# Where the fetched rows' sums begin and leave, and when the odd mixer's weights are asked for, in a two-layer decoder trunk

## The chip, the cores and the metric

The kernel runs on one core of a Trainium2 chip. The metric is the device time of one execution in microseconds (us). Repeated executions of this kernel agree within a few tenths of a microsecond, so a change of 0.2% (3 us) can be told from no change.

## The reference, cut to what matters

Two pre-norm residual layers over 256 tokens of width 1024. Layer 0 mixes tokens by attention and retention, layer 1 by a gated short convolution. After each mixer comes PEER, an expert mixer: every token picks 8 x 16 = 128 of 16,384 experts, and each expert is one row of `u` and one row of `v`.

```python
for layer in range(2):
    xn = rmsnorm(h, norm_mix[layer])
    h = h + (attn_retention_mixer if layer == 0 else short_conv_mixer)(xn, ...)
    h = h + peer(rmsnorm(h, norm_ffn[layer]), peer_w_q[layer], ..., peer_u[layer], peer_v[layer])
return rmsnorm(h, final_norm)

def peer(t, w_q, sub_keys, u, v):
    ...                                   # product keys: eidx (token, 128 experts), gate
    hid = gelu(einsum('td,tkd->tk', t, u[eidx]))
    return einsum('tk,tkd->td', gate * hid, v[eidx])
```

## The kernel before, in words

**Two ways through PEER.** The last 160 tokens (`TD`) take a dense way: all 16,384 experts are run over them, 128 tiles of `u` and then 128 tiles of `v`, each tile 128 experts by 1024 floats, and a matrix of gates zeroes what a token did not choose. The first 96 tokens (`TG`) take a fetched way: class `Gather` reads exactly the chosen rows from HBM by indirect DMAs on the POOL queue (L966). One such DMA fetches one row of 1024 floats for each of 128 partitions. 96 tokens x 128 experts are 96 DMAs of rows of `u` and 96 of rows of `v` in each layer; the text calls the result of one such DMA "a row". Partitions 0 to 95 hold one token each. Partitions 96 to 127 (`TG:`) help out: in the first 32 rows they work for tokens 0 to 31, in the next 32 for tokens 32 to 63, in the last 32 for tokens 64 to 95.

**The sums of the fetched way.** VectorE (DVE) consumes rows in order (`consume`, called from `step`). A row of `v` is scaled and added into `acc[q]`, q = 0, 1, 2 for the three blocks of 32 rows (L985 for the first row, L987 and L988 for the first of a later block, L991 for all others). `acc[q][:TG]` begins on `acc[q-1][:TG]`. The helpers' sums, `acc[q][TG:]`, are carried to their tokens' place in `acc[0]` by a small DMA on the POOL queue (`part`, L1003), the third of them after the very last row. Then `fold` (L999) adds `acc[2][:TG]` and `acc[0][:TG]` into the residual `h[:TG]`, two DVE instructions, the second of which waits for that DMA.

**The v stage** is the loop `for i in range(NK)` at the end of `peer`: 128 steps, one tile of `v` (`pv`) each, eight PSUM banks `vo[b]` that collect the dense tokens' output. In 33 steps the raw tile is multiplied in float32 (L1484, 16 matmul instructions). In the 95 steps of `SPL` it is split beforehand into a rounded part `vhi` on ScalarE (ACT, L1369) and a rest `vlo` on DVE (L1376), three steps ahead, with the gated activations split likewise (L1442, L1443, L1450), and the step is L1488 and L1490. Tile 126 is raw, tiles 123, 124, 125 and 127 are split.

**The pace of the rows.** In each step `ga.step()` adds `ga.rate` to a credit and consumes a row per whole credit; after each consume the next row is asked for, up to six ahead. The rate is chosen so that `(16 - end) * late` rows are left when step 114 begins, and from there it is `late` rows a step:

```python
late = 1.0 if last else 0.8
end = 3.5 if last else 7.5
ga.rate = (ga.TOTAL - ga.c - (16 - end) * late) / (NK - 16.0)
```

`last` is layer 1, the last one.

**The end of the v stage in layer 0.** At step 123 (`NK - 5`) all rows must be consumed and `fold` is called on DVE. At step 126 (`NK - 2`), ahead of that step's own products, PE adds the transposed `h[:TG]` to the banks as eight products with the identity (L1476), and ACT copies them to `XT` (L1479), the transposed residual. After step 127 `fold(b)` takes the dense tokens' sums out of the banks (ACT L1497, DVE L1498), and `Folded.folded` makes the odd mixer's input from `XT`.

**The end in layer 1** is `Final.folded`: eight `fold(b)`, sixteen transposes back to token rows (L506), squares on ACT (L586), the gather's `fold` on DVE (L999), two copies of the dense tokens of the first half into `h` (L603), gains (L583), the norm (L365 to L377), the scaling (L592, L590) and four stores (L593). It calls `ga.fold()` in its middle.

**The stream of weights.** `Stream` keeps eight raw buffers for all weight tiles of the program, in one order: `wq`, `pu`, `pv` of layer 0, then the odd mixer's `ow_in` and `ow_out`, then layer 1. A tile is asked for when the tile eight places earlier has been handed out (`free(self.nl - RAW)`), so the odd mixer's first tiles (numbers 128 and on, counted from the first tile of `pv`) are asked for in the last steps of layer 0's v stage. All loads go out on SP's queue (L131) but for every second `pv` tile, which goes on ACT's. In the program each load waits for the release of the buffer that it goes into. Instructions of one engine or queue run in the order in which the program writes them.

The functions that the diff touches, before:

Of the kernel before, what the change touches and what calls it, by code (L numbers as in the profile page):

```python
# [19 lines left out]
P = 128  # L20
# [8 lines left out]
NK = 128  # L29
# [40 lines left out]
def shape_constants():  # L70
    c = np.zeros((P, C_N), np.float32)
    c[:, C_ID:C_ID + P] = np.eye(P)
    c[:, C_IO:C_IO + P] = np.arange(P)[None, :]
    c[:, C_ONE] = 1.0
    c[:, C_ST:C_ST + TK] = np.array(STARTS)[None, :]
# [29 lines left out]
class Stream:  # L105
# [58 lines left out]
    def ahead(self, extra=0):  # L164
        n = len(self.srcs)
        while True:
            if self.nl < n and self.free(self.nl - RAW):
                self._load()
            elif self.ns < min(n, self.nu + extra + self.depth()) and self.ns < self.nl:
                self._split()  # L170
            else:
                return

    def parts(self):

        self._split()
        while self.nl < len(self.srcs) and self.free(self.nl - RAW):
# [14 lines left out]
def trunk_kernel(ctx, tc, x, small, cst, mcst, ew_in, ew_out, ow_in, ow_out, wq, keys, pu, pv, pun, gains, out):  # L192
# [363 lines left out]
    class Final(Sums):  # L556
# [12 lines left out]
        def folded(self, XT, fold, ga):  # L569


# [7 lines left out]
            def row(a):  # L579
                return fq[a] if a > 1 else h[:, 0, a * 512:(a + 1) * 512]  # L580

            def gained(a):
                v.tensor_tensor(part(a), row(a), self.g[:, a % 2 * 512:(a % 2 + 1) * 512], OP.mult)  # L583

            def square(a):
                act.activation(junk, row(a), AF.Square, accum_out=self.w[:, a // 2, a % 2:a % 2 + 1])  # L586
# [10 lines left out]
            for a in (2, 3, 0, 1):  # L597
                back(fq[a], XT, a // 2, a % 2)
            for a in (2, 3):
                square(a)  # L600
            ga.fold()
            for a in range(2):
                v.tensor_copy(h[TG:, 0, a * 512:(a + 1) * 512], fq[a][TG:, :])  # L603
# [12 lines left out]
            gained(1)  # L616
# [54 lines left out]
    def even_mixer(before, norm):  # L671
        with tc.tile_pool(name=nm("mix"), bufs=1) as mp, tc.tile_pool(name=nm("mix2"), bufs=2) as mp2:
# [152 lines left out]
            at(2, lambda: nc.sync.dma_start(M[:, M_MASK:], mcst[:, M_MASK:]))  # L825
            at(14, lambda: load_keys(0))
# [103 lines left out]
    class Gather:  # L930
# [5 lines left out]

        TOTAL = 2 * STEPS
# [31 lines left out]
        def consume(self):  # L969
# [592 lines left out]
```

## Time and profile before

| | us |
|---|---|
| median of 3 runs | 1496.39 (1496.20 to 1496.56) |
| profiled execution | 1497.11 |
| its span, first to last instruction | 1495.3 |
| PE busy | 1436.5 (96%) |
| DVE busy | 1247.0 (83%) |
| ACT busy | 760.6 (51%) |
| POOL busy | 730.8 (49%) |
| mean DMA traffic | 356 GB/s over the span |

The profiled execution is 0.72 us above the median, and 1.8 us of it lie outside its span. A busy PE includes matmuls that overlap or run at a lower clock, so stages are read by what ends their waits. In the profile's lines a time from the span's start and a duration come first, then engine, line of the kernel, operation, output<-inputs, shapes and count; in brackets stands the engine's idle time before it and what ended it.

### The profile page before, as it was taken

The page shows a single profiled execution, that of the slowest core. Times are in us where ns is not written, and L with a number is a line of the kernel's source. Part 1 is how long each engine was busy: PE and PEld are TensorE (multiplying, and loading weights), DVE is VectorE, ACT ScalarE, POOL GpSimd, SP SyncE. Part 2 cuts the span into 40 slices and gives each one's busy share as a digit, 9 for nine tenths or more (in the row PEclk, how much of TensorE's full clock was granted, in tenths as well). Part 3 has the DMA queues.
Part 4 walks back from the last instruction along what each step waited for, and adds up shares of the span by engine and source line. Part 5 has one row for each costly group of instructions (what it writes and reads, how often), then busy time and mean ns, then how long its engine had stood idle before and what let it go on. Part 6 is the DMA issues. An engine that isn't in the chain of part 4 may idle for free.

```text
span 1495.3 us, 30076 instructions
## 1 busy us (share of the span) xinstructions
PE 1436.5 (96%) x11158; PEld 1334.2 (89%) x11172; DVE 1247.0 (83%) x2469; ACT 760.6 (51%) x1825; POOL 730.8 (49%) x514
## 2 busy tenths in 40 slices
PE   9999999999999999999989999999999999999995
PEld 5667999999999999888879799999999999988885
DVE  5637999879998888888867589996899978888888
ACT  6556512257875544445564363212888745444453
POOL 6754545446665344343235364454566643434342
PEclk9999999999999999999999999999999999999998
DMA  8545899999999999999946578999999999999995
GB/s 318 198 148 201 307 385 407 394 409 403 405 405 408 405 398 409 409 399 408 398 171 234 181 257 321 408 409 397 408 405 401 406 407 405 396 409 409 400 394 224
DMA packets 147570, 532.99 MB, mean 356 GB/s; under 512 B 16992, under 2 KB 17248, under 8 KB 147424
## 3 DMA queue, kind: packets, MB, share of 16 engines
q1 hardware_dynamic: 72144, 258.36, 45.1%
q0 software_dynamic: 56704, 205.07, 34.8%
q10 hardware_dynamic: 18576, 67.64, 11.5%
q8 instruction: 88, 1.44, 0.4%
q14 instruction: 58, 0.48, 0.1%
HBM read 528.34 MB, written 1.05 MB: 354 GB/s over the span
## 4 chain that ended last, share of the span: by engine, by line
PE 38%; DMA 18%; DVE 17%; issue 16%; POOL 8%; ACT 2%; another core or an unknown queue 0%; SPq 0%; POOLq 0%; DVEq 0%; ACTq 0%
PE hid L1358 17%; DMA raw<-pv 8%; POOL rows L966 5%; PE hid L258 4%; DMA rows<-pun,ig 3%; DMA grow<-pun,ig 3%; DVE rows L976 3%; POOL grow L966 2%; DMA rows<-pv,ig 2%; PE vo L1488 2%; DMA raw<-pu 2%; PE ea L290 2%; PE hid L264 2%; PE ea L291 2%; PE ea L292 1%
## 5 line engine op out<-in xcount | busy, mean ns | idle before, releaser
L1358 PE MATMUL hid<-xf,raw 128*128 128x160 f32 x3392 | 485.3, 300 | 6.8 <-DMA raw<-pu 4.2
L1358 PEld LDWEIGHTS hid<-xf,raw 128*128 128x128 f32 x3392 | 465.4, 190 | 9.7 <-issue 6.2
L1369 ACT CAST vhi<-raw 128x1024 fp32r<-128x1024 f32 x190 | 198.5, 1045 | 266.4 <-DMA raw<-pv 192.4
L1376 DVE TENSOR_TENSOR vlo<-raw,vhi 128x1024 bf16<-128x1024 f32 x190 | 231.9, 1223 | 81.1 <-ACT vhi L1369 62.9
L1488 PE MATMUL vo<-ko,vhi 128*128 128x320 f32 x1520 | 270.4, 320 | 26.8 <-DVE ko L1450 26.3
L966 POOL DMA_INDIRECT rows<-pv,ig x128 | 188.6, 1474 | 214.6 <-DVE gacc L991 174.0
L1488 PEld LDWEIGHTS vo<-ko,vhi 128*128 128x128 f32 x1520 | 224.2, 188 | 36.5 <-DVE ko L1450 35.9
L966 POOL DMA_INDIRECT rows<-pun,ig x128 | 170.6, 1333 | 134.3 <-DVE rows L976 59.5
L148 POOL TENSOR_TENSOR lo<-raw,hi 128x1024 bf16<-128x1024 f32 x70 | 168.3, 2415 | 86.2 <-ACT hi L146 83.2
L976 DVE SCALAR_TENSOR_TENSOR rows<-rows,xg 128x1024 f32<-128x1024 f32 x128 | 155.3, 1219 | 21.1 <-DMA rows<-pun,ig 19.8
L1391 ACT ACTIVATE hg<-hid 128x160 f32<-128x160 f32 (+14 forms) x240 | 62.3, 264 | 194.5 <-PE hid L1358 171.8
L991 DVE SCALAR_TENSOR_TENSOR gacc<-rows,ghid,gacc 128x1024 f32<-128x1024 f32 x124 | 158.7, 1279 | 2.1 <-DMA rows<-pv,ig 1.3
L1484 PE MATMUL vo<-hg,raw 128*128 128x160 f32 x1056 | 158.7, 303 | 1.0 <-DVE hg L1394 1.0
L966 POOL DMA_INDIRECT grow<-pv,ig x64 | 91.0, 1421 | 122.9 <-DVE gacc L991 113.1
L1484 PEld LDWEIGHTS vo<-hg,raw 128*128 128x128 f32 x1056 | 147.0, 192 | 1.5 <-DVE hg L1394 1.5
L1490 PE MATMUL vo<-hb,vlo 128*128 128x160 bf16 x1520 | 138.1, 234 | 0.4 <-DVE vlo L1376 0.4
L1308 ACT ACTIVATE ko<-ko,idxT 128x128 f16<-128x128 f16 x320 | 101.8, 390 | 52.6 <-DVE ko L1294 52.4
L966 POOL DMA_INDIRECT grow<-pun,ig x64 | 80.3, 1255 | 79.4 <-DVE grow L976 45.6
L1490 PEld LDWEIGHTS <-vlo 128*128 128x128 bf16 x1520 | 100.5, 98 | 20.1 <-DVE vlo L1376 0.9
L146 ACT CAST hi<-raw 128x1024 fp32r<-128x1024 f32 x100 | 102.7, 1047 | 30.2 <-PE hid L258 18.5
L258 PE MATMUL hid<-x,hi 128*128 128x256 f32 x800 | 107.4, 287 | 0.5 <-DVE cg L904 0.5
L1311 ACT ACTIVATE ko<-ko,idxT 128x128 f16<-128x128 f16 x320 | 101.1, 387 | 0.0
(247 smaller groups left out, 2086.7 us busy)
## 6 DMA issues: line engine op xcount, KB each, us to landing
raw<-pu SPq DMA_DIRECT2D x212, 512.0 KB
raw<-pv SPq DMA_DIRECT2D x128, 512.0 KB
raw<-pv ACTq DMA_DIRECT2D x128, 512.0 KB
raw<-wq SPq DMA_DIRECT2D x32, 512.0 KB
raw<-ew_in SPq DMA_DIRECT2D x28, 512.0 KB
raw<-ow_in SPq DMA_DIRECT2D x24, 512.0 KB
hg<-pu SPq DMA_DIRECT2D x22, 512.0 KB
raw<-ew_out SPq DMA_DIRECT2D x8, 512.0 KB
```

What stands on the lines that cost most here:

```text
L146: self.nc.scalar.copy(hi, t)
L148: eng.tensor_tensor(lo, t, hi.bitcast(F32), OP.subtract)
L258: pe.matmul(ps[:, :S], hi[:, k * P:(k + 1) * P], A2[:, k, s_, :], start=k == 0 and s_ == 0, stop=False)
L966: gp.indirect_dma_start(self.row(s_), None, table, bass.IndirectOffsetOnAxis(IG[:, 0, s_ % STEPS:s_ % STEPS + 1].bitcast(U32), 0))
L976: v.scalar_tensor_tensor(r, r, 1.0, XG[:, q % 2, :], op0=OP.mult, op1=OP.mult, accum_out=w)
L991: v.scalar_tensor_tensor(self.acc[q], r, w, self.acc[q], op0=OP.mult, op1=OP.add)
L1358: pe.matmul(ps[:, :TD], w[k], XF[:, k, :], start=k == 0, stop=k == ND - 1)
L1369: act.copy(whi[j], raw)
L1376: v.tensor_tensor(wlo[j], raw, whi[j].bitcast(F32), OP.subtract)
L1484: pe.matmul(vo[b][:, :TD], w[:, b * P:(b + 1) * P], HG[:, i, :], stop=False, **m)
L1488: pe.matmul(vo[b][:, :2 * TD], hi[:, b * P:(b + 1) * P], hs, stop=i == NK - 1, **m)
L1490: pe.matmul(vo[b][:, :TD], lo[:, b * P:(b + 1) * P], hb, stop=i == NK - 1, **m)
```

## The change

Five things, in both layers unless it says otherwise:

1. The sum of the fetched rows begins on the residual: the first row of block 0 is now handled as those of blocks 1 and 2 (two instructions), with `h[:TG]` as what it is added to.
2. The helpers' third DMA is gone. The first two are folded in 8 rows after block 2 begins: one DVE instruction adds `acc[0][:64]` into `acc[2][:64]`. The helpers' last block stays in `acc[2][TG:]`, and a constant 128 x 128 matrix `own` with a one at (p, p) for p < 96 and at (p, p - 32) for p >= 96 brings it to its tokens inside a product. It is loaded once, in the even mixer, into the place of a scratch tile.
3. Layer 0: the eight products that put the first 96 tokens into the banks take `acc[2]` and `own` instead of `h` and the identity; they stand ahead of step 127 instead of step 126, and `fold` at step 123 is gone. `late` is 1.0 and `end` 5.5, so the rows may run to a later step.
4. Layer 0: only two of the odd mixer's tiles are asked for until all rows have been consumed (`st.stop`).
5. Layer 1: the tail goes by halves of the columns. Per half, one product of `own` with 512 columns of `acc[2]` starts a bank with the first 128 tokens' fetched sums, four products of `XT` with the identity add the dense tokens (the first 96 columns of `XT` are zeroed on POOL at step 24), and four transposes make the other 128 tokens. All later steps read the banks, so the `fold` and the copies are gone. `end` is 4.5.

```diff
 class Stream:
+        self.stop = len(srcs)
...
     def ahead(self, extra=0):
-            if self.nl < n and self.free(self.nl - RAW):
+            if self.nl < self.stop and self.free(self.nl - RAW):
                 self._load()
...
     def parts(self):
-        while self.nl < len(self.srcs) and self.free(self.nl - RAW):
+        while self.nl < self.stop and self.free(self.nl - RAW):
...
+    def owners():
+        xv["own"] = pers.tile([P, P], F32, tag="z", name="own")
+        nc.sync.dma_start(xv["own"], cst[:, C_N:])
...
     class Final: def folded(self, XT, fold, ga):
             for b in range(ND):
                 fold(b)
-            for a in (2, 3, 0, 1):
-                back(fq[a], XT, a // 2, a % 2)
-            for a in (2, 3):
-                square(a)
-            ga.fold()
-            for a in range(2):
-                v.tensor_copy(h[TG:, 0, a * 512:(a + 1) * 512], fq[a][TG:, :])
-            self.mean0(1)
+            for ch in range(2):
+                pe.matmul(fq[ch], xv["own"], ga.acc[2][:, ch * 512:(ch + 1) * 512], start=True, stop=True)
+                for b in range(4):
+                    c = slice(b * P, (b + 1) * P)
+                    pe.matmul(fq[ch][:, c], XT[:, ch * 4 + b, :P], ident, start=False, stop=True,
+                              skip_group_check=True)
+                    pe.transpose(fq[2 + ch][:, c], XT[:, ch * 4 + b, P:], ident)
+                if ch == 0:
+                    square(0)
+                    gained(2)
+                    square(2)
+                    gained(0)
+                    self.mean0(1)
+                    self.mean0(0)
+            square(3)
+            gained(1)
             self.root(1)
-            gained(2)
+            square(1)
             gained(3)
+            self.root(0)
             self.rstd(1)
-            for a in range(2):
-                square(a)
-            self.mean0(0)
-            self.root(0)
             put(2, v)
-            gained(0)
             put(3, act)
-            gained(1)
             self.rstd(0)
             put(0, v)
             put(1, act)
...
     class Gather: def consume(self):
-            elif j == 0:
-                v.tensor_scalar(self.acc[0], r, w, None, op0=OP.mult)
             elif j % SUB == 0:
-                v.scalar_tensor_tensor(self.acc[q][:TG], r[:TG], w[:TG], self.acc[q - 1][:TG], op0=OP.mult, op1=OP.add)
+                so_far = self.acc[q - 1] if q else h[:, 0, :]
+                v.scalar_tensor_tensor(self.acc[q][:TG], r[:TG], w[:TG], so_far[:TG], op0=OP.mult, op1=OP.add)
                 v.tensor_scalar(self.acc[q][TG:], r[TG:], w[TG:], None, op0=OP.mult)
-                self.part(q - 1)
+                if q:
+                    self.part(q - 1)
+                if q == 2:
+                    self.later[s_ + 8] = self.fold
...
-            if s_ == self.TOTAL - 1:
-                self.part(2)
...
         def fold(self):
-            for a in (2, 0):
-                v.tensor_tensor(h[:TG, 0, :], self.acc[a][:TG], h[:TG, 0, :], OP.add)
+            a = self.acc
+            v.tensor_tensor(a[2][:2 * SUB], a[0][:2 * SUB], a[2][:2 * SUB], OP.add)
...
     def peer, the v stage:
-            late = 1.0 if last else 0.8
-            end = 3.5 if last else 7.5
+            late = 1.0
+            end = 4.5 if last else 5.5
+            st.stop = min(first + NK + 2, len(srcs))
...
+                if i == 24 and last:
+                    gp.memset(XT[:, :, :TG], 0.0)
...
-                    if i == NK - 2 and not last:
-                        pe.matmul(vo[b][:, 2 * TD:2 * TD + TG], h[:, 0, c], ident[:, :TG], **m)
-                if i == NK - 2 and not last:
+                    if i == NK - 1 and not last:
+                        pe.matmul(vo[b][:, 2 * TD:2 * TD + TG], ga.acc[2][:, c], xv["own"][:, :TG], **m)
+                w = st.next()
+                if i == NK - 1 and not last:
                     for b in range(ND):
                         act.copy(XT[:, b, :TG], vo[b][:, 2 * TD:2 * TD + TG])
-                w = st.next()
...
-                if i == NK - 5 and not last:
-                    assert ga.c == ga.TOTAL
-                    ga.fold()
+                if ga.c == ga.TOTAL and not done:
+                    done.append(i)
+                    st.stop = len(srcs)
```

More of the change, by code (lines that the diff above doesn't have):

```diff
@@ L74, in shape_constants @@
     c[:, C_ONE] = 1.0
+    for p in range(P):
+        c[p, C_N + (p if p < TG else p - SUB)] = 1.0
     c[:, C_ST:C_ST + TK] = np.array(STARTS)[None, :]
@@ L577, in part @@
                 return xs[:, a // 2, a % 2 * 512:(a % 2 + 1) * 512]
-            def row(a):
-                return fq[a] if a > 1 else h[:, 0, a * 512:(a + 1) * 512]
             def gained(a):
-                v.tensor_tensor(part(a), row(a), self.g[:, a % 2 * 512:(a % 2 + 1) * 512], OP.mult)
+                v.tensor_tensor(part(a), fq[a], self.g[:, a % 2 * 512:(a % 2 + 1) * 512], OP.mult)
             def square(a):
-                act.activation(junk, row(a), AF.Square, accum_out=self.w[:, a // 2, a % 2:a % 2 + 1])
+                act.activation(junk, fq[a], AF.Square, accum_out=self.w[:, a // 2, a % 2:a % 2 + 1])
             def put(a, eng):
@@ L825, in even_mixer @@
             at(2, lambda: nc.sync.dma_start(M[:, M_MASK:], mcst[:, M_MASK:]))
+            at(4, owners)
             at(14, lambda: load_keys(0))
@@ L1454, in peer @@
                 row_rest()
+            done = []
             for i in range(NK):
@@ L1498, in fold @@
                 v.tensor_tensor(XT[:, b, TG:], vo[b][:, :TD], XT[:, b, TG:], OP.add)
-            assert ga.c == ga.TOTAL
+            assert done and done[0] < NK - 1, done
             norm.folded(XT, fold, ga)
@@ L1509, in trunk_kernel @@
             (nc.scalar if th else nc.sync).dma_start(h[:, th, :], x[th])
-        nc.sync.dma_start(C[:, P:], cst[:, P:])
+        nc.sync.dma_start(C[:, P:], cst[:, P:C_N])
         v.memset(Z, 0.0)
```

2 lines of the change are left out of this document (1 added, 1 removed).

## The prediction

> **What bounds the kernel now.** I read the page first, then the two places that the diff touches: the last 30 us of each layer's v stage. On the page:
>
> ```profile
> span 1495.3 us, 30076 instructions
> ...
> PE 38%; DMA 18%; DVE 17%; issue 16%; POOL 8%; ACT 2%; another core or an unknown queue 0%; SPq 0%; POOLq 0%; DVEq 0%; ACTq 0%
> ```
>
> No single engine carries the chain that ended last, so a gain must be looked for where the change sits. Stretches of layer 0's v stage and its end (us; busy time and count of PE, PEld, DVE, ACT, POOL; granted clock; DMA share; GB/s):
>
> ```profile
> 720.00:740.00 20.00, 19.45 (x168) 18.30 (x167) 18.49 (x18) 9.12 (x12) 5.97 (x4) 1.00 1.03 407
> 740.00:750.00 10.00, 8.34 (x72) 7.59 (x70) 8.48 (x8) 6.89 (x10) 0.54 (x1) 1.00 0.96 364
> 750.00:753.50 3.50, 0.00 (x0) 0.00 (x0) 1.26 (x2) 0.00 (x0) 0.00 (x0) 0.93 0.48 146
> 753.50:757.00 3.50, 3.48 (x16) 3.48 (x17) 1.33 (x2) 1.57 (x7) 0.00 (x0) 0.50 0.40 131
> ```
>
> Up to 740 the DMA engines are full (share 1.03, 407 GB/s): the stage goes at the pace of the transfers, and a tile or a row of 128 x 4 KB costs 524,288 B / 407 GB/s = 1.29 us. Then PE stands still for a whole 3.5 us stretch and runs the next one at clock 0.50. PE in order of time, steps 125 (its end), 126 and 127 of layer 0:
>
> ```profile
> 749.26 0.73 PE L1490 MATMUL vo<-hb,vlo 128*128 128x160 bf16 x8
> 753.52 3.73 PE L1476 MATMUL vo<-cst,h 128*128 128x96 f32 x16 [3.53 <-DVE h L999]
> 757.04 3.74 PE L1484 MATMUL vo<-hg,raw 128*128 128x160 f32 x16
> 760.51 1.44 PE L1488 MATMUL vo<-ko,vhi 128*128 128x320 f32 x8
> 761.79 0.73 PE L1490 MATMUL vo<-hb,vlo 128*128 128x160 bf16 x8
> ```
>
> The stage ends at 761.79 + 0.73 = 762.5. Why PE waits stands on DVE, POOL and ACT, one view each:
>
> ```profile
> 744.50 1.22 DVE L1376 TENSOR_TENSOR vlo<-raw,vhi 128x1024 bf16<-128x1024 f32 x1
> 745.64 1.28 DVE L991 SCALAR_TENSOR_TENSOR gacc<-rows,ghid,gacc 128x1024 f32<-128x1024 f32 x1
> 746.84 1.22 DVE L1376 TENSOR_TENSOR vlo<-raw,vhi 128x1024 bf16<-128x1024 f32 x1
> 747.98 1.21 DVE L999 TENSOR_TENSOR h<-gacc,h 96x1024 f32<-96x1024 f32 x1
> 752.24 1.22 DVE L999 TENSOR_TENSOR h<-gacc,h 96x1024 f32<-96x1024 f32 x1 [3.05 <-DMA gacc<-gacc]
> 753.38 1.22 DVE L1376 TENSOR_TENSOR vlo<-raw,vhi 128x1024 bf16<-128x1024 f32 x1
> ```
>
> ```profile
> 730.24 1.68 POOL L966 DMA_INDIRECT rows<-pv,ig  x1 [0.66 <-DVE gacc L991]
> 747.21 0.54 POOL L1003 DMA_DIRECT2D gacc<-gacc  x1 [15.29 <-DVE gacc L991]
> ```
>
> ```profile
> 747.04 1.05 ACT L1369 CAST vhi<-raw 128x1024 fp32r<-128x1024 f32 x1 [1.62 <-DMA raw<-pv]
> ```
>
> The last row is consumed at 745.64, between the splits of tiles 124 and 125, which by the code is step 122. The helpers' third DMA goes out at 747.21, the second `fold` waits 3.05 us for it on DVE, the products on PE wait 3.53 us for that `fold`, and tile 127's `vlo` (753.38), whose tile was there at 747.04, is queued behind it.
>
> **Layer 0, part by part.** The third DMA and both `fold` instructions leave this place, so the 3.53 us go. What ran at clock 0.50 after them is cheaper at 1.00. Layer 1's end shows both prices, in PE's order of time:
>
> ```profile
> 1474.92 2.38 PE L1484 MATMUL vo<-hg,raw 128*128 128x160 f32 x16
> 1478.24 1.44 PE L1488 MATMUL vo<-ko,vhi 128*128 128x320 f32 x8 [0.94 <-DVE ko L1450]
> 1479.52 0.73 PE L1490 MATMUL vo<-hb,vlo 128*128 128x160 bf16 x8
> 1481.46 2.35 PE L506 MATMUL fq<-cst,xg 128*128 128x128 f32 x16 [1.21 <-DVE xg L1498]
> ```
>
> Step 126 took 757.04 to 760.51, 3.47 us, against 2.38 here: 1.09 less. The eight products are 16 instructions, 753.52 to 757.04, 3.52 us; at full clock I price them by L506's sixteen, 2.35 us: 1.17 less (96 columns instead of 128 make it no dearer, and 16 weight loads keep it from being much cheaper). Together 3.53 + 1.09 + 1.17 = 5.8 us.
>
> What is late next: the products read `acc[2]`, so they wait for the last row. At step 114, 6.8 rows were left at 0.8 a step, now 10.5 at 1.0: the last is consumed 10.5 steps on, at step 124 instead of 122. DVE's queue then reads: row 191, row 192, `vlo` and rest of tile 127. If a row is late, tile 127 is late behind it, and PE waits. Layer 1 before already runs at 1.0 a step and has two rows beside tile 127; there PE waits 0.94 us for that rest, and I take 0.9 lost. The bounds are 0, since two consumes fewer stand at the very end than in layer 1, and 0.9 + three further odd-mixer tiles that take the last rows' bandwidth, 3 x 1.29 = 3.9, so 4.8.
>
> In exchange two rows fewer have been moved when tile 125 is needed. In a stage at the transfers' pace that puts PE's step 125 up to 2 x 1.29 = 2.6 us earlier, or 0 earlier if DVE sets the pace (18.49 of 20 us busy in the first stretch above). I take the middle, 1.3.
>
> Holding back the odd mixer's tiles I price at nothing. On SP's queue in order of time before:
>
> ```profile
> 743.82 0.92 SPq L131 DMA_DIRECT2D raw<-ow_in  x2
> ```
>
> On that queue stand nothing but loads, and each waits for its buffer. Writing them later in the program puts nothing new ahead of them, so they still leave when the buffers come free. By the Trainium skill ("DMA: Bandwidth & Descriptors", section "Issuing engines are not separate DMA queues") transfers of all queues share the same 16 engines and interleave; by that rule tiles that really stayed back would hand their time to the rows, which is the second rival.
>
> Layer 0: -5.8 + 0.9 - 1.3 = -6.2, with ends -1.0 (-5.8 + 4.8) and -8.4 (-5.8 - 2.6). The odd mixer's own start takes the gain over: its first tiles were asked for at 743.82 and before.
>
> **Layer 1's tail.** DVE, ACT and SP before, each in order of time:
>
> ```profile
> 1478.11 2.60 DVE L991 SCALAR_TENSOR_TENSOR gacc<-rows,ghid,gacc 128x1024 f32<-128x1024 f32 x2
> 1480.62 1.94 DVE L1498 TENSOR_TENSOR xg<-vo,xg 128x160 f32<-128x160 f32 x8
> 1482.47 2.47 DVE L999 TENSOR_TENSOR h<-gacc,h 96x1024 f32<-96x1024 f32 x2
> 1484.97 1.31 DVE L603 COPY h<-fq 32x512 f32<-32x512 f32 x2
> 1486.31 0.15 DVE L365 TENSOR_SCALAR nw<-nw 128x1 f32<-128x1 f32 x1
> 1486.50 1.29 DVE L583 TENSOR_TENSOR ko<-fq,xf 128x512 f32<-128x512 f32 x2
> ...
> 1490.20 0.16 DVE L373 SCALAR_TENSOR_TENSOR nw<-nw 128x1 f32<-128x1 f32 x1
> ...
> 1491.10 0.48 DVE L592 TENSOR_SCALAR ko<-ko,nw 128x512 f32<-128x512 f32 x1
> ```
>
> ```profile
> 1482.15 0.60 ACT L586 ACTIVATE xb<-fq 128x512 bf16<-128x512 f32 x1 [0.69 <-PE fq L506]
> 1482.65 0.19 ACT L586 ACTIVATION_READ_ACCUMULATOR xb<-fq 128x1 f32 x1
> ```
>
> ```profile
> 1489.11 3.31 SPq L593 DMA_DIRECT2D out<-ko  x4
> ```
>
> From the first L1498 add to the end of the span it is 1495.3 - 1480.62 = 14.7 us, and DVE sets it: 2.47 of `fold` and 1.31 of copies stand in it, both gone. Now PE sets the first half. From the first add, in us: its result is there at 0.3; the product with `own` streams 512 columns in two passes, by L1484's 298 ns for 160 columns (2.38 / 8) some 0.95; then four times two pass instructions and one transpose, 3 x 147 ns (2.35 / 16), 1.76. So the first half is done at 3.0, the second at 5.7. Then DVE has the longest row: two gains (0.65 each) to 7.0, the norm of one half 0.9 (1490.20 to 1491.10) to 7.9, scaling 0.49 to 8.4, the other norm to 9.3, scaling to 9.8. ACT squares twice meanwhile (0.79 each, to 7.5 with the roots) and makes the last scaling by 10.0. Last store issued by 10.5; before, it was at 1489.11 + 3.31 = 1492.42, and 2.9 us followed. End at 13.4 against 14.7: -1.3. No row shows a product of 512 columns; at half or double its price of 0.95 the two of them move the tail by -1.0 or +1.9.
>
> With `end` at 4.5 one more row comes ahead of step 114, so the last tiles land up to 1.29 us later; but the adds waited for the two consumes at 1478.11, of which one is gone from there. I take 0.3 lost, between -0.3 and +1.3. Layer 1: -1.3 + 0.3 = -1.0, from -2.6 (-1.3 - 1.0 - 0.3) to +1.9 (-1.3 + 1.9 + 1.3).
>
> **At nothing.** The first row's second instruction and the mid-stage `fold` are two DVE instructions of at most 1.3 us a layer, under the transfers' pace; with that cover gone, 2.6 a layer. The zeroing on POOL stands in front of one indirect DMA, of which six are ahead. `own` is one load on SP's queue behind weight loads of the even mixer. The mid-stage `fold` waits for a DMA issued eight rows earlier, long landed.
>
> **Sum.** -6.2 - 1.0 = -7.2. The profiled execution, 1497.11 us (1495.3 of span), would come to 1489.9; it stands 0.72 above the median, so from the median 1496.39 I get **1489.2**. A difference of 0.2%, 3 us, is about what a measurement can tell from none.
>
> **Rivals.** *The new wait replaces the old (10%).* If the last row lands so late that PE stands idle about as long as the 3.53 us before, the clock falls again, and only the tail's 1.0 is left: 1495.4. For it: SP goes on sending odd-mixer tiles beside the last rows, which layer 1 did not have. Against it: with rows at 1.0 a step layer 1 lost only 0.94. The Trainium skill ("TensorE: Matmul & The Clock Gate", "What's actually happening") has the clock halve after an idle window of some 3.4 us that runs freely; 3.53 idle and 0.50 after it agree, and by the rule an idle time just under the window may still be let off.
>
> *The hold does hold (16%).* If the tiles stay away until step 124, the two issued at 743.82, ahead of tile 127's landing at 747.04, no longer share its bandwidth: 2 x 1.29 = 2.6 more, 1486.6. Against it: the queue argument above.
>
> *Slower: rows starve behind the tiles (8%).* The last row is now asked for three steps later, each of a tile and a row (2.6 us), so at 730.24 + 7.8 = 738. If the six rows outstanding come at 3.5 us each, the last lands at 759; consume 1.28, products at half clock 3.5, step 127 slowed to some 3: the stage ends at 767, 4.5 after 762.5, less 1.0: 1499.9. From 3.0 us a row on (landing at 756, end 764) there is no gain in layer 0. Against it: layer 1 consumed two rows in 2.60 us at 1478.11 without a wait between them.
>
> **Chances.** The forecast has 66%. Its ends all on one side would be 1485.4 (-8.4 - 2.6) and 1497.3 (-1.0 + 1.9); both are unlikely, and the nearest row, layer 1's 0.94, speaks for the faster half. Faster by over 3 us: forecast and hold, 82%; within 3 us: the new wait, 10%; slower by more: the starving rows, 8%. The range leaves those last two out. It takes in a last row late by the full 3.9 (1489.2 + 3.9 = 1493.1) with 1.4 of a dearer tail, and the hold (1486.6) with 2.1 of the better ends: 1484.5 to 1494.5.
>
> **What would show it.** In layer 0: no 3.53 us before the eight products, clock 1.00 across steps 126 and 127, the last consume two steps later, loads of `ow_in` leaving at the buffers' release as before, a v stage that ends about 6 us earlier. In layer 1: no L999 or L603 in the tail, 13 to 14 us from the first L1498 add to the end. Wrong would be an idle PE of over 3 us before the products of step 127, or an odd mixer whose first tiles come late.

## The result, and the profile after

The changed kernel takes **1489.98 us** (median of 11 executions, 1488.19 to 1494.92), the kernel before 1495.91 us in the same comparison (11 executions, 1493.42 to 1496.56). The medians differ by 5.9 us; the ratio is 0.9964, 95% interval 0.9956 to 0.9972, which is 4.2 to 6.6 us less. The forecast was 1489.2 us, 7.2 less, in a range of 1484.5 to 1494.5. Executions of one kernel scatter more than the three first ones showed: 27 of the kernel before, in one of the comparisons below, lie between 1493.33 and 1499.00 us. Differences of a microsecond or two between two profiles can be that scatter. The profiled execution of the changed kernel took 1490.58 us with a span of 1488.8 us, 6.5 us below the span before.

The end of layer 0's v stage, in the same stretches as before (busy time and count of PE, PEld, DVE, ACT, POOL; granted clock; DMA share; GB/s):

```profile
740.00:750.00 10.00, 6.88 (x57) 6.02 (x57) 7.75 (x8) 6.40 (x9) 0.00 (x0) 1.00 1.03 410
750.00:753.50 3.50, 2.48 (x19) 2.24 (x19) 2.24 (x3) 0.40 (x3) 0.00 (x0) 1.00 0.86 337
753.50:757.00 3.50, 3.06 (x28) 2.76 (x27) 3.41 (x6) 2.25 (x11) 0.00 (x0) 1.00 0.76 263
```

The stretch without any PE work is gone, the clock stays at 1.00, and the DMA engines are full until 750 (share 1.03) and at 0.86 and 0.76 after it. PE in order of time, from the end of step 125 on; then DVE:

```profile
748.80 0.73 PE L1503 MATMUL vo<-hb,vlo 128*128 128x160 bf16 x8 [1.77 <-DVE vlo L1385]
749.37 2.38 PE L1497 MATMUL vo<-hg,raw 128*128 128x160 f32 x16
752.77 2.02 PE L1489 MATMUL vo<-own,gacc 128*128 128x96 f32 x16 [1.02 <-DVE gacc L1002]
754.58 1.42 PE L1501 MATMUL vo<-ko,vhi 128*128 128x320 f32 x8
755.84 0.73 PE L1503 MATMUL vo<-hb,vlo 128*128 128x160 bf16 x8
```

```profile
747.53 1.22 DVE L1385 TENSOR_TENSOR vlo<-raw,vhi 128x1024 bf16<-128x1024 f32 x1
748.88 1.28 DVE L1002 SCALAR_TENSOR_TENSOR gacc<-rows,ghid,gacc 128x1024 f32<-128x1024 f32 x1
751.43 1.28 DVE L1002 SCALAR_TENSOR_TENSOR gacc<-rows,ghid,gacc 128x1024 f32<-128x1024 f32 x1 [1.26 <-DMA rows<-pv,ig]
752.63 1.22 DVE L1385 TENSOR_TENSOR vlo<-raw,vhi 128x1024 bf16<-128x1024 f32 x1
```

The eight products (L1489 now) still wait, but for the last row and only 1.02 us, where it was 3.53 us for the `fold`. The stage ends at 756.6 instead of 762.5. On POOL and on SP's queue:

```profile
736.49 1.68 POOL L975 DMA_INDIRECT rows<-pv,ig  x1 [0.66 <-DVE gacc L1002]
```

```profile
735.05 21.67 SPq L134 DMA_DIRECT2D raw<-ow_in  x10
```

The last row is asked for at 736.49, and DVE's wait for it ends at 751.43, 14.9 us later. Loads of `ow_in` leave from 735.05 on: nothing is held back in time.

The tail of layer 1, one view each of DVE, PE and SP's queue:

```profile
1475.91 1.94 DVE L1512 TENSOR_TENSOR xg<-vo,xg 128x160 f32<-128x160 f32 x8 [0.74 <-ACT xg L1511]
```

```profile
1476.29 1.12 PE L602 MATMUL fq<-gacc,own 128*128 128x512 f32 x2 [0.26 <-DVE xg L1512]
1477.25 0.38 PE L605 MATMUL fq<-cst,xg 128*128 128x128 f32 x2
...
1478.58 1.02 PE L602 MATMUL fq<-gacc,own 128*128 128x512 f32 x2
...
1480.66 0.27 PE L607 MATMUL fq<-cst,xg 128*128 128x128 f32 x1
```

```profile
1483.77 2.14 SPq L597 DMA_DIRECT2D out<-ko  x4
```

From the first add (1475.91) to the end of the span it is 12.9 us, against 14.7 before.

Stage by stage (lengths in the two profiles, after minus before, us, between the first matmul of a stage and that of the next; layer 1's v stage ends with its last product, and the tail begins there): u stage of layer 0 +0.9, v stage of layer 0 -6.6, odd mixer -0.2, u stage of layer 1 +1.6, v stage of layer 1 +0.4, tail -2.3. A second trace of the same instructions, that of the kernel without the hold below, gives +2.0, -8.2, 0.0, +1.6, +0.5 and -2.3. Both u stages, which the prediction had at nothing, got longer. Where it happens in layer 0, one view each (DVE before, DVE after, PE after):

```profile
435.99 0.82 DVE L985 TENSOR_SCALAR gacc<-grow,ghid 128x1024 f32<-128x1024 f32 x1
```

```profile
435.48 1.27 DVE L995 SCALAR_TENSOR_TENSOR gacc<-grow,ghid,h 96x1024 f32<-96x1024 f32 x1
436.76 0.75 DVE L996 TENSOR_SCALAR gacc<-grow,ghid 32x1024 f32<-32x1024 f32 x1
```

```profile
442.23 1.35 PE L1367 MATMUL hid<-xf,raw 128*128 128x160 f32 x8 [0.84 <-DVE hg L1403]
```

The first row of `v` is consumed while the u stage still runs. It now costs DVE 1.27 + 0.75 = 2.02 us instead of 0.82, 1.20 more, and PE soon after waits for DVE, which it did not do there before.

### The profile page after: what moved, and what is told of

Its sections match the earlier page's. It is cut to its first block, busy times and chain, and to the rows that moved or that the text cites. A ratio compares the mean times of both kernels' runs of the same rounds, so it can differ in the third digit from the quotient of the medians.

```text
span 1488.8 us, 30108 instructions
## 1 busy us (share of the span) xinstructions
PE 1438.1 (97%) x11184; PEld 1334.8 (90%) x11184; DVE 1246.5 (84%) x2467; ACT 761.3 (51%) x1825; POOL 744.9 (50%) x513
## 3 DMA queue, kind: packets, MB, share of 16 engines
HBM read 528.40 MB, written 1.05 MB: 356 GB/s over the span
## 4 chain that ended last, share of the span: by engine, by line
PE 54%; issue 17%; POOL 11%; DMA 9%; DVE 7%; ACT 2%; POOLq 0%; DVEq 0%; ACTq 0%; SPq 0%
PE hid L1367 30%; POOL rows L975 7%; PE hid L261 5%; DMA raw<-pu 4%; DMA raw<-pv 3%; POOL grow L975 3%; PE hid L267 2%; PE G L1327 2%; DMA rows<-pv,ig 2%; PE ea L295 2%; PE vo L1501 2%; PE ea L294 2%; PE ea L293 2%; DVE gacc L1002 1%; PE vo L1497 1%
## 5 line engine op out<-in xcount | busy, mean ns | idle before, releaser
L1367 PEld LDWEIGHTS hid<-xf,raw 128*128 128x128 f32 x3392 | 467.1, 191 | 10.5 <-issue 5.6
L975 POOL DMA_INDIRECT rows<-pv,ig x128 | 192.5, 1504 | 209.2 <-DVE gacc L1002 180.0
L975 POOL DMA_INDIRECT grow<-pv,ig x64 | 99.7, 1558 | 122.8 <-DVE gacc L1002 110.9
```

Of the source, the lines that this page charges most:

```text
L975: gp.indirect_dma_start(self.row(s_), None, table, bass.IndirectOffsetOnAxis(IG[:, 0, s_ % STEPS:s_ % STEPS + 1].bitcast(U32), 0))
L1367: pe.matmul(ps[:, :TD], w[k], XF[:, k, :], start=k == 0, stop=k == ND - 1)
```

## The experiments

The theory after the result: the gain is layer 0's stall and what the low clock made of the work behind it; the tail's gain is real but is spent again by the first row's second instruction in the u stages; the hold does nothing. The rivals: the gain is mostly the clock; or the new place and pace of the rows; or the hold after all; or the u stages' loss is scatter between executions. Each kernel was compared in 5 rounds with the kernel before; traces of one execution each are read beside the medians.

**One layer each.** First the changed layer 0 with the old layer 1, then the old layer 0 with the changed layer 1. One line of each edit stands for the rest; the second argument asks for all the old parts, and `norm.own` is true in layer 1 alone:

```diff
-            ga = Gather(hp)
+            ga = Gather(hp, norm.own)
...
```
```diff
-            ga = Gather(hp)
+            ga = Gather(hp, not norm.own)
...
```

> Layer 0 as in the changed kernel, layer 1 wholly as before (third DMA, fold into h, old tail, end 3.5). Theory (the stall before layer 0's step 126, and the low clock after it, is most of the gain): v stage of layer 0 ends 5 to 7 us earlier than before, total -6 +- 1 us; layer 1's tail 15.1 us from PE's last product to the end, as before. Rival (the tail is most of it): -2 us or less.

> Layer 0 wholly as before, layer 1 as in the changed kernel (sums on the residual, own, tail in halves, end 4.5). Theory: -1 to -2.5 us, tail from PE's last product to the end 12.8 us instead of 15.1; layer 0's PE still idle 3.5 us before the eight products. Rival (the tail is most of the gain): -4 us or more.

Measured: layer 0 alone 1490.92 us, ratio 0.9963 (0.9949 to 0.9977); layer 1 alone 1496.26 us, 1.0001 (0.9991 to 1.0010), against 1496.50 before. That is -5.6 and -0.2 us, together -5.8 of the whole change's -5.9. Layer 0 carries it; layer 1 alone missed the 1 to 2.5 us expected of it. In its trace the tail is shorter by the same 2.3 us as in the whole change, and its u stage is 1.4 us longer, though that comes from an early place of the stage, where the granted clock is 0.50 for 3.4 us (a low-clock spell, from 953.9), and not from the first row.

That trace also shows another execution of the old end of layer 0. PE and DVE:

```profile
744.34 1.44 PE L1513 MATMUL vo<-ko,vhi 128*128 128x320 f32 x8 [1.98 <-DVE ko L1472]
745.62 1.22 PE L1515 MATMUL vo<-hb,vlo 128*128 128x160 bf16 x8
746.57 2.48 PE L1513 MATMUL vo<-ko,vhi 128*128 128x320 f32 x8
748.85 0.85 PE L1515 MATMUL vo<-hb,vlo 128*128 128x160 bf16 x8
...
753.43 2.02 PE L1501 MATMUL vo<-cst,h 128*128 128x96 f32 x16 [1.95 <-DVE h L1018]
755.29 2.37 PE L1509 MATMUL vo<-hg,raw 128*128 128x160 f32 x16
```

```profile
752.15 1.22 DVE L1018 TENSOR_TENSOR h<-gacc,h 96x1024 f32<-96x1024 f32 x1 [3.27 <-DMA gacc<-gacc]
```

The DMA is waited for as before (3.27 us), but a row came late earlier on, step 125 ended later, and PE stood only 1.95 us; products and step 126 ran at full speed (2.02 and 2.37). The low clock fell on steps 124 and 125 instead. So 3.53 us and a half clock behind it were one execution's share, not a constant of the kernel before.

**The clock by itself.** The kernel before, with 52 matmuls of zeros ahead of the waiting products:

```diff
+                if i == NK - 2 and not last:
+                    for _ in range(52):
+                        pe.matmul(vo[7][:, 2 * TD + TG:2 * TD + 2 * TG], Z[:, :P], Z[:, :TG], **m)
```

> The kernel before with 52 small matmuls of zeros on PE ahead of the eight products of step 126, into columns of a bank that nothing reads. They fill the 3.53 us of waiting. Theory (the idle time pulls the clock down): products at about 2.1 to 2.4 us instead of 3.7, step 126 2.4 instead of 3.7, granted clock 1.00, total -2.3 +- 0.7 us. Rival (the products are slow because ACT empties the banks beside them, not by the clock): no change in their time, total 0 to +0.5.

```profile
749.54 2.37 PE L1472 MATMUL vo<-z 128*128 128x96 bf16 x52
754.03 2.02 PE L1479 MATMUL vo<-cst,h 128*128 128x96 f32 x16 [2.11 <-DVE h L999]
755.89 2.37 PE L1487 MATMUL vo<-hg,raw 128*128 128x160 f32 x16
```

Products and step 126 take 2.02 and 2.37 us instead of 3.73 and 3.74, so the low clock, and not ACT's copies beside them, had made them slow. But the median is 1495.64 us, 0.9994 (0.9985 to 1.0003): 0.9 us at the best estimate, missing the 1.6 to 3.0 expected from the profile of before (1.09 + 1.17). By the mean granted clock of the whole span that profile was not an unusually slow draw: 0.995 in it, 0.9938 on average over the 27 executions of the kernel before, and 0.9953 over the 11 with the zeros. In the trace with the zeros a low spell of 3.4 us stands at the odd mixer's start instead (763.3), and that stage is 0.6 us longer than before; where the rest of the saving went is not shown.

**The place by itself.** The kernel before, with `fold` at the end of step 125 and the products ahead of step 127; third DMA, pace and tail as they were:

```diff
-                    if i == NK - 2 and not last:
+                    if i == NK - 1 and not last:
...
-                if i == NK - 2 and not last:
+                if i == NK - 1 and not last:
...
-                if i == NK - 5 and not last:
+                if i == NK - 3 and not last:
```

> The kernel before with one thing changed: layer 0's fold is called at the end of step 125 instead of 123, and the eight products stand ahead of step 127 instead of 126. Third DMA, old sums, old pace stay. Theory that it is the place of the wait: tile 127's split is no longer behind the fold, step 126 runs while the DMA lands, PE waits about 1 us or less, clock stays 1.00: -4 to -5.5 us. Rival (the DMA and the two folds have to go, which the 0-1 matrix does): PE waits 2.5 us or more, gain under 2 us.

PE, then DVE:

```profile
755.85 1.92 PE L1476 MATMUL vo<-cst,h 128*128 128x96 f32 x16
```

```profile
753.94 1.22 DVE L999 TENSOR_TENSOR h<-gacc,h 96x1024 f32<-96x1024 f32 x1 [1.36 <-DMA gacc<-gacc]
```

PE does not wait ahead of the products any more; DVE still waits 1.36 us for the DMA. 1493.95 us, 0.9982 (0.9973 to 0.9991), so 2.5 us less, where 4 to 5.5 were expected: a bit under half of the gain comes from the later place alone. As the pace turns out to add nothing that can be measured, the rest is left for the third DMA and the two `fold` instructions; that is by difference, no run takes them away alone.

**The pace by itself.** The changed kernel with the old pace of rows in layer 0 (first), and with `late` 1.0 but `end` 7.5 (second). Both have all rows consumed earlier than the changed kernel:

```diff
-            late = 1.0
-            end = 4.5 if last else 5.5
+            late = 1.0 if last else 0.8
+            end = 4.5 if last else 7.5
```

```diff
-            end = 4.5 if last else 5.5
+            end = 4.5 if last else 7.5
```

> The changed kernel with layer 0's old pace, late 0.8 and end 7.5. Again the last row at step 122. Theory: within 1 us of the changed kernel; PE waits for no row at step 127. If the pace of 1.0 is part of the gain: 2 us slower or more than the changed kernel.

> The changed kernel with end 7.5 instead of 5.5 in layer 0: two rows more before step 114, the last one consumed at step 122. If the last rows are late because they are asked for late: PE's waits at steps 125 and 127 (1.77 and 1.02 us) go, the v stage ends 1 to 2.5 us earlier. If the stage goes at the pace of the transfers alone: two tiles land later for it, the end stays within 0.7 us.

Measured: 1489.66 us, 0.9966 (0.9956 to 0.9977), and 1491.21 us, 0.9970 (0.9960 to 0.9980). Neither can be told from the changed kernel's 0.9964. The trace of the old pace has no wait before the products:

```profile
753.57 1.92 PE L1489 MATMUL vo<-own,gacc 128*128 128x96 f32 x16
```

but its step 125 ended 261.5 us after the start of the v stage, against 260.1 in the changed kernel and 258.5 in the second trace of the same instructions. So in single traces the pace brings step 125 forward by 1.4 to 3.0 us and costs the new wait of 1.0; that little is left of it is what the medians say, and their intervals reach 1.5 us to either side. The second one's profiled execution (1494.89 us, well above its median) cannot decide between its two expectations, but it shows what an unlucky row does, on DVE and then on PE:

```profile
744.21 1.28 DVE L1002 SCALAR_TENSOR_TENSOR gacc<-rows,ghid,gacc 128x1024 f32<-128x1024 f32 x1 [2.56 <-DMA rows<-pv,ig]
```

```profile
747.26 1.58 PE L1501 MATMUL vo<-ko,vhi 128*128 128x320 f32 x8 [4.26 <-DVE ko L1460]
```

One row 2.56 us late makes 4.26 us of idle PE, since the split and the rest of the next tile stand behind it on DVE.

**The hold.** The changed kernel without it; then with a hold that works in time: a copy of 128 KB of `acc[2]`, whose result nobody reads, on SP's queue ahead of the third `ow_in` tile. It waits for the last row, and everything behind it on that queue waits too.

```diff
-            st.stop = min(first + NK + 2, len(srcs))
```
```diff
                     done.append(i)
+                    if not last:
+                        nc.sync.dma_start(ga.acc[0][2 * SUB:TG, :], ga.acc[2][TG:, :])
```

> The changed kernel without st.stop: the odd mixer's tiles are asked for as before. Theory (the hold moves nothing, since SP's queue holds only loads that wait for buffers): same time as the changed kernel, -5.5 to -7 us against before, loads of ow_in leave at the same points. Rival (the hold keeps the tiles off the rows): 1.3 to 2.6 us slower than the changed kernel.

> The changed kernel with a hold that acts in time: a 128 KB copy of acc[2][96:] to an unused place of acc[0] stands on SP's queue between the second and the third tile of the odd mixer, so that queue waits for the last row's consume. If the tiles 130 to 133 delay the last rows: DVE waits for rows (0.83, 1.29 and 1.26 us) shrink by 2 us or more in all, v stage of layer 0 ends 1.5 to 3 us earlier. If not: the v stage ends as in the changed kernel, and the odd mixer's third tile comes later, by 0 to 2 us.

Without `st.stop`: 1490.11 us, 0.9963 (0.9950 to 0.9976), the same as with it. Every engine's instructions stand in the same order with the same waits in the two programs, so the hold changes nothing at all, and the new wait stands in this trace too:

```profile
752.15 2.02 PE L1488 MATMUL vo<-own,gacc 128*128 128x96 f32 x16 [1.03 <-DVE gacc L1002]
```

With the copy: 1487.96 us, 0.9957 (0.9944 to 0.9971). SP's queue, DVE and PE of that kernel:

```profile
734.95 2.66 SPq L134 DMA_DIRECT2D raw<-ow_in  x2
751.15 0.59 SPq L1509 DMA_DIRECT2D gacc<-gacc  x1
751.83 12.39 SPq L134 DMA_DIRECT2D raw<-ow_in  x9
```

```profile
748.52 2.60 DVE L1002 SCALAR_TENSOR_TENSOR gacc<-rows,ghid,gacc 128x1024 f32<-128x1024 f32 x2
```

```profile
751.44 1.92 PE L1489 MATMUL vo<-own,gacc 128*128 128x96 f32 x16
```

Between 737.6 and 751.15 no tile leaves on SP's queue; the last two rows are there when DVE wants them, PE does not wait, and the odd mixer is as long as before. DVE's waits for rows shrink by 1.4 us, where 2 were expected. In all five traces at the new pace without a hold that works, those of later kernels included, PE waits 0.87 to 1.05 us ahead of the products; in the three with it, not at all. The prediction's rival of a hold that holds priced this at 2.6 us. The medians of these two kernels differ by 2.15, their means by 0.95 (1489.79 and 1488.84), and the intervals overlap, so from these two alone the gain is not shown.

**The u stages.** The changed kernel with the first row as one instruction again; the residual comes in on POOL in the v stage instead (an add for tokens 0 to 63, a copy for 64 to 95). First alone, then with the working hold:

```diff
+            elif j == 0:
+                v.tensor_scalar(self.acc[0], r, w, None, op0=OP.mult)
...
+                    self.later[s_ + 6] = self.residual
...
+        def residual(self):
+            a = self.acc
+            gp.tensor_tensor(a[0][:2 * SUB], a[0][:2 * SUB], h[:2 * SUB, 0, :], OP.add)
+            gp.tensor_copy(a[0][2 * SUB:TG], h[2 * SUB:TG, 0, :])
         def fold(self):
             a = self.acc
-            v.tensor_tensor(a[2][:2 * SUB], a[0][:2 * SUB], a[2][:2 * SUB], OP.add)
+            v.tensor_tensor(a[2][:TG], a[0][:TG], a[2][:TG], OP.add)
```

> The changed kernel, but the first row of v is again one DVE instruction (0.82 us) instead of two (1.27 + 0.75), in both layers; the residual comes in later, by an add and a copy on POOL into acc[0] six rows after block 2 begins, and the mid-stage fold adds 96 instead of 64 partitions. Theory (DVE sets PE's pace where the first row is consumed, so the second instruction costs its 1.2 us there in each layer): the u stages lose the 1.0 to 1.6 us that the changed kernel's had over the kernel before, PE's idle 0.84 us at the first row is gone, total 1 to 2.5 us below the changed kernel. Rival (those differences are scatter from execution to execution): u stages as in the changed kernel, total the same within 1 us.

> The same with the hold that acts in time (a 128 KB copy of acc[2][96:] on SP's queue ahead of the odd mixer's third tile). Expected if both act and add: 3 to 4 us below the changed kernel, about 1486.5 us; v stage of layer 0 without a wait of PE ahead of the eight products. If they do not add: as the better one alone.

Missed: 1503.12 us, 1.0052 (1.0038 to 1.0065), and 1499.43 us, 1.0031 (1.0020 to 1.0042), both slower than before. The u stages did lose their extra time (layer 0 -0.1 and layer 1 -0.2 against before). But POOL's queue, in the first of the two, whose trace is of its fastest execution (1497.93 us):

```profile
673.05 2.51 POOL L1009 TENSOR_TENSOR gacc<-gacc,h 64x1024 f32<-64x1024 f32 x1
680.01 1.62 POOL L1010 COPY gacc<-h 32x1024 f32<-32x1024 f32 x1 [4.45 <-DMA rows<-pv,ig]
681.90 13.37 POOL L975 DMA_INDIRECT rows<-pv,ig  x1 [0.27 <-POOL gacc L1010]
695.58 0.94 POOL L975 DMA_INDIRECT rows<-pv,ig  x1 [0.30 <-issue]
```

and the stretch of 30 us around it there and then in the changed kernel:

```profile
670.00:700.00 30.00, 26.19 (x219) 24.44 (x217) 23.46 (x20) 16.12 (x20) 22.86 (x8) 1.00 0.91 329
```

```profile
670.00:700.00 30.00, 28.98 (x241) 27.10 (x240) 27.77 (x26) 16.09 (x21) 18.34 (x10) 1.00 1.02 404
```

The add and the copy, which itself waits 4.45 us, stand ahead of the row requests; the next request takes 13.37 us, others 0.9 to 1.9, and the traffic falls from 404 to 329 GB/s. Why that one request takes so long is not shown.

So the same once more, with the residual on DVE: one add of all 96 tokens, 12 rows into block 2, in the v stage, and `fold` as in the changed kernel. First without the working hold, then with it:

```diff
-                    self.later[s_ + 6] = self.residual
+                    self.later[s_ + 12] = self.residual
...
         def residual(self):
             a = self.acc
-            gp.tensor_tensor(a[0][:2 * SUB], a[0][:2 * SUB], h[:2 * SUB, 0, :], OP.add)
-            gp.tensor_copy(a[0][2 * SUB:TG], h[2 * SUB:TG, 0, :])
+            v.tensor_tensor(a[2][:TG], h[:TG, 0, :], a[2][:TG], OP.add)
```

> The changed kernel, but the first row of block 0 is again one DVE instruction over all 128 partitions, and the residual is added into acc[2] by one DVE instruction 12 rows into block 2, in the v stage. Theory (the second instruction of the first row costs 1.2 us a layer because it stands in the u stage, where PE waits for DVE, while in the v stage one more DVE instruction lies under the transfers' pace): the jump of 1.2 us at the first row of v is gone in both u stages, the v stages are as long as in the changed kernel, total 1 to 2.5 us below it, about 1487.5. Rival (the POOL variants lost time because the residual comes in during the v stage at all, and POOL's queue had no part in it): u stages short, but v stages 3 to 6 us longer, total near 1495 to 1500. Rival (the u stage is held by something else): no jump removed, total as the changed kernel, 1490.

> The same with the copy on SP's queue that really keeps the odd mixer's tiles back until the last row of v is consumed. If the two gains add up (1.2 us a layer from the u stages, 2 us from the hold): 1485 to 1486.5, no wait of PE ahead of the eight products in layer 0, below both kernels and below the kernel with the hold alone. Rival (late residual and hold collide at the end of the v stage of layer 0): as the variant without the hold, 1487.5 or more.

The first row is one instruction of 0.82 us again, and PE's waits for DVE around it are gone in both layers. The u stages are +0.2 and -0.2 us from before without the hold, where the changed kernel has +0.9 and +1.6; with the hold +0.1 and +0.8, and the 0.8 come from an earlier place of the stage, where a low-clock spell stands (3.4 us from 947.4). Layer 0's v stage pays nothing for it that can be seen (-7.2 and -9.0 us against before; the changed kernel's instructions -6.6 and -8.2, the working hold alone -8.5). So the work on POOL, not the late residual, had made the two kernels above slow. The times are another matter: 1489.64 us, 0.9966 (0.9954 to 0.9978), missing the expected 1487.5 and not to be told from the changed kernel; with the hold 1487.86 us, 0.9949 (0.9936 to 0.9962), above the expected 1485 to 1486.5. In both traces layer 1's v stage is longer (+2.1 and +1.5 us against before, +0.4 in the changed kernel). The place in the first of them, on DVE and PE:

```profile
1460.68 1.28 DVE L1003 SCALAR_TENSOR_TENSOR gacc<-grow,ghid,gacc 128x1024 f32<-128x1024 f32 x1 [2.37 <-DMA grow<-pv,ig]
```

```profile
1463.72 2.50 PE L1506 MATMUL vo<-ko,vhi 128*128 128x320 f32 x8 [3.08 <-DVE ko L1465]
```

A row that is not there yet stops DVE, and PE stands for 3.08 us at step 123. The row comes at the transfers' pace, whatever the u stage saved: that is how I read it, but whether such a wait is the rule or the bad luck of two traces stays open. The kernel with `end` 7.5 in layer 0, which has no late residual, is 1.4 us longer in this stage of its trace as well.

The kernel with both is the fastest measured, below before by its whole interval, but its interval overlaps the changed kernel's (0.9956 to 0.9972). The hold itself stands firmer when executions are put together. Below 1488.19 us, the fastest of the changed kernel's eleven, lie 4 of 6 with the copy against 1 of 16 of the two programs of the same instructions without it, and 4 of 5 against 2 of 12 where the first row is one instruction. Its size is less sure: by medians and means 1 to 3 us.

## Why the prediction was right, and where its steps were off

**The old stall goes: right.** The terms from profile to profile, in us: the wait 3.53 becomes 1.02, so -2.5, predicted -3.53 + 0.9. Step 126 takes 2.38 instead of 3.47, -1.1 as predicted. The products take 1.8 (752.77 to 754.58) instead of 3.52, -1.7, predicted -1.17: 16 instructions with 96 columns are a quarter cheaper than the 2.35 us of the row with 128, just as 96 is to 128; I had used it unscaled, expecting the weight loads to hold it up. Step 125 ends 1.1 us earlier in the stage, predicted 1.3. Together -6.4, and the v stage's -6.6 is that and 0.2 in which the modelled end of step 125 overlaps step 126. With the odd mixer's -0.2 it makes -6.9, against -6.2 forecast. That step 125 came so close is luck: in the second trace of the same instructions it ends 2.7 us earlier than before.

**But the profile of before was one draw.** The 3.53 us and the half clock behind it were read as the kernel's. In the trace with the old layer 0 and the new tail the same code lost 1.95 us at full clock, and keeping the clock up saved at most 2.2 us (the interval's end, 0.9985). The median gain of layer 0 alone is 5.6 us all the same. What is steady in the three traces of the old end, the one with the zeros included, is where the products start: 264.7, 265.0 and 265.3 us into the stage. Where the wait was short, step 125 had been late (263.1 us into the stage, before 261.2, changed kernel 260.1).

**The new wait: right in place and size** (row 192 ahead of tile 127's split, 0.9 predicted, 1.02 measured, 0.87 to 1.05 in five traces). It is the price of the new pace: a term of -1.3 and one of +0.9, of which the medians at the two paces show no remainder.

**The hold at nothing: right, and for the reason given.** The rival that it holds was false for this code, yet its price was not far off: a hold that works in time is worth 1 to 3 us. The Trainium skill ("DMA: Bandwidth & Descriptors", section "Issuing engines are not separate DMA queues") says that transfers of all queues interleave on the same engines. That tiles not sent then leave their time to the rows is drawn from it, and the run with the copy agrees: DVE does not wait for the last row, against 1.26 us.

**Starving rows** stayed away, but not by much: 14.9 us from the last request to its landing, six rows outstanding, is 2.5 us a row, and the rival decided from 3.0.

**The tail: mechanism right, size off.** 14.7 to 12.9 instead of 13.4. The product with 512 columns is 1.0 to 1.1 us (priced 0.95), and the four groups of `XT` products and transposes behind it take 1.3 us (1477.25 to 1478.58), not 1.76: first half done at 2.7 instead of 3.0, second at 5.0 instead of 5.7. That no row shows a product of 512 columns was an oversight: the profile of before has instructions of that shape (L290 and L291, 128x512 f32, 560 and 394 ns on average), so 0.8 to 1.1 us for two. The last store is issued 10.0 us after the first add (10.5 forecast), and 2.9 follow as before.

**The step that failed is "At nothing".** It put the first row's second instruction "under the transfers' pace", as if it were in the v stage. It is in the u stage, and there DVE has no slack. The prediction did price two such instructions without that cover, at 2.6 us a layer, but gave the case no chance. A row that the prediction should have asked for, the stretch around it before, and the same after:

```profile
425.00:455.00 30.00, 29.95 (x255) 29.41 (x255) 29.96 (x48) 24.44 (x97) 20.54 (x13) 1.00 1.02 405
```

```profile
425.00:455.00 30.00, 28.97 (x241) 28.22 (x241) 29.92 (x47) 23.33 (x93) 19.87 (x12) 1.00 1.02 401
```

DVE was busy 29.96 of 30 us: 1.20 us more of it is PE's loss, 1.0 us of PE work less in these 30 us. In layer 0 all six traced kernels that have the two instructions fall back 1.2 to 1.5 us against before at that place, and none of the seven others does by more than 0.1. In layer 1 it is four of six; the other two had fallen back 1.3 and 1.7 us earlier in the stage, beside low-clock spells (from 948.9 and 953.9), and lost nothing more there. That early loss is not the change's: the kernel with the zeros, whose layer 1 is the old one, has such a spell too (from 954.5) and falls back 1.4 us. So the tail's gain and the u stage's loss stand against each other in layer 1, and alone it measured -0.2 us, between -1.3 and +1.5. The loss is shown in the traces, not in the total: without the second instruction, with the residual on DVE, the median stayed at 1489.64 us.

Span for span the change is -6.5 instead of -7.2: the u stages 2.4 worse, the rest of layer 1 0.9 better (0.4 lost in its v stage, the tail 2.3 shorter from the last product on, 1.8 of it after the first add), layer 0's v stage and odd mixer 0.7 better, and 0.2 ahead of them. The medians, at -5.9, are another 0.6 short, which is less than the scatter of single executions. So the forecast's nearness is in part luck: a missed loss of 2.4 us stands against 1.6 of gains that were sized too small, in one draw of each kernel.

## What to carry to other kernels

A cover holds for a place, not for an instruction: before an addition is priced at nothing, ask for the busy share of its own engine in the stretch where it runs (here 29.96 of 30 us), not in the stage to which it belongs by name. Holding back a load in program order did nothing here, where it waits for its buffer anyway; to hold it in time, something on its queue had to wait for the right event. And a stall read from one trace is one draw: a second trace of the same code, here from a variant that left it alone, shows how much of it is the kernel's.

## What the runs showed of the hardware

An idle time well under 3.5 us can come before a halved clock. In the run of layer 1 alone PE stood 1.98 us (until 744.34), ran the first eight instructions of step 124 at full speed, and was slow over the next three groups (2.48 us for eight instructions that else take 1.42). In the windows view of that trace the low clock fills one stretch of 3.41 us, the second below:

```profile
742.27:745.68 3.41, 1.43 (x10) 1.24 (x10) 3.41 (x5) 2.63 (x4) 0.00 (x0) 1.00 0.77 294
745.68:749.10 3.42, 3.42 (x19) 3.22 (x19) 3.21 (x3) 1.50 (x3) 0.53 (x1) 0.50 0.97 371
749.10:752.51 3.41, 2.38 (x24) 2.08 (x22) 0.36 (x1) 0.00 (x0) 0.00 (x0) 1.00 0.81 240
752.51:755.92 3.41, 2.49 (x21) 2.49 (x22) 2.24 (x3) 1.99 (x9) 0.00 (x0) 1.00 0.15 23
```

The 1.98 us lie within the first stretch, where PE is busy for 1.43 us, 42%. The 1.95 us in the same trace (751.48 to 753.43) are shared by the third and the fourth, 70% and 73% busy, and had no such effect; nor had 2.11 us behind the zero matmuls. The 3.08 us at the end of layer 1 above were followed by a slow step at once (2.50 us at 1463.72): PE was busy for 0.38 of the 3.42 us before the spell, which begins at 1463.69.

The Trainium skill ("TensorE: Matmul & The Clock Gate", section "What's actually happening") names an idle window of about 3.4 us that runs freely. The traces agree that it runs freely: between 15 and 1472 us of all 14, every low spell lasts 3.41 us or a whole multiple, and the spells of one trace begin whole multiples of 3.41 us apart. They do not agree that the window has to be idle throughout. Cut by that grid, they have 25 windows at full clock in which PE was busy for 44.5% or less, and 23 of these were followed by a low one; of the other 5,920 three were, at 54% and 68%, all at the odd mixer's start. PE's ends are modelled, so the limit between 42% and 46% is an estimate from these traces.
